# Moving the results of two expert quads by one block in a mixture-of-experts stage

## The chip, the cores and the metric

The kernel runs on one core of a Trainium2 chip. The metric is the device time of one execution in microseconds; the kernel before has a median of 2238.95 us over 3 runs (2238.46 to 2247.0).

## The reference

The reference is one layer of an encoder over 2048 tokens of width 1024: projections, a gated DeltaNet and an attention mixer, an output projection, and then a mixture of 32 experts with a final layer norm. Only the experts matter here:

```
hid = silu(xb @ w1[e]) * (xb @ w3[e])      # per block of tokens of expert e, 1024 -> 256
ys  = (hid @ w2[e]) * row_w                # 256 -> 1024, times the token's weight
out = segment_sum(ys, row_tok)             # two experts per token are added up
x   = layer_norm(ALPHA * x + gt2 * out, ln2_g, ln2_b)
```

Each token has two experts of one of four groups, so there are 4096 rows of work, spread unevenly over the 32 experts.

## The kernel before, in words

All stages before the experts (projections, attention, recurrence, output projection, routing) are outside the change. Routing leaves, for each expert, a list of its tokens; d_x1 holds the residual into which the experts' results are added, and d_h the experts' input.

The expert stage (`experts`, line 2049) works on two kinds of places. A *block* is up to 128 tokens of one expert. There are 40 places for blocks: 14 lone ones (`singles`) and 13 pairs of blocks of one expert (`pairs`), in the order lone, pair, lone, pair and so on, so that block n is a lone one when n is 0 mod 3, the first of a pair at 1 and the second at 2. A *quad* is four experts with at most 32 tokens each, put side by side in 128 rows; there are `QS` = 3 quads.

`blocks` (line 1996) writes the order of all engines out by hand (`manual_schedule`); GpSimd (POOL) and the three compute engines follow it as it stands. In its step n it issues the gather of block n + 3 (`gather`), the first half of block n's hidden product (`block_hid` 0), the transpose of the gated product of block n - 1 (`block_gt`), splits of weights, the second half of the hidden product, its activation, the transposes of block n + 1's rows (`block_x`), more splits, and then the output product of block n - 1 (`block_y`) and its addition to d_x1 (`block_out`, line 1892). A split (line 67) turns a weight tile into a high and a low part, on ScalarE and VectorE; it frees the raw tile, and the weights of the unit after next are then requested on SP's queue (`load_unit`). A lone block has three splits in its step (two of w1/w3 for the next unit and one of its own w2), the first of a pair has one (its w2), the second of a pair has two.

The output product goes into `yo`, which has two PSUM buffers of half a row width; VectorE scales it into `ye`, which has two buffers for blocks and quads together (line 1887 for blocks, 1960 for quads). From `ye` an indirect DMA with addition goes to d_x1; all of these write the same tensor, so each waits until the one before has landed.

The parts of a quad hang in this order at steps that the list `QA` gives, three numbers per quad (`quads`, line 1967): the first half of the hidden product (line 1932), the second half with the activation, and the output (line 1959). From these follow: the gather of the quad's rows three steps before the first (`quad_x`), its transposes one step before (`quad_xt`), the transpose of the gated product one step behind the second (`quad_gt`), and two additions to d_x1 behind the output (`quad_out`, line 1963), the second of them in the step after. The four raw weight tiles `qraw` are single: w1/w3 of the first half, of the second half, w2, and then the next quad's first half go into the same tiles, each set requested on SP's queue in two portions of two experts, in the step of the part that used the tiles last and in the step behind it.

```
QA = (13, 18, 21, 24, 27, 30, 33, 36, 39)
QL = ((0, 1), (2, 3))
```

Functions:

Of the kernel before, what the change touches and what calls it, by code (L numbers as in the profile page):

```python
# [44 lines left out]
SB = 2 * NP + NS  # L45
POS = 80
FEW, QS = 32, 3
QA = (13, 18, 21, 24, 27, 30, 33, 36, 39)
QL = ((0, 1), (2, 3))
TD = (0, 2)  # L50

# [5 lines left out]
class Layer:  # L57
# [1909 lines left out]
    def quads(self):  # L1967
# [3 lines left out]
        def put(n, f, *a):  # L1971
            at.setdefault(n, []).append(lambda: f(*a))
# [6 lines left out]
        for q in range(QS):  # L1979
            n = QA[3 * q:3 * q + 3]  # L1980
            put(n[0] - 3, self.quad_x, q)
# [200 lines left out]
```

## Time and profile before

| what | value |
|---|---|
| median of 3 runs | 2238.95 us (2238.46 to 2247.0) |
| profiled execution | 2234.89 us |
| its span (first to last instruction) | 2233.0 us |
| mean granted TensorE clock | 0.961 |
| TensorE, VectorE, ScalarE, GpSimd busy | 90%, 73%, 56%, 38% |

Busy times come from one profiled execution. The expert stage lies from about 1707 us (first gathers) to 2179 us; behind it come the loads of d_x1 and the final layer norm, to the end. PE is TensorE, DVE is VectorE, ACT is ScalarE, POOL is GpSimd and SP the queue that loads weights; L and a number is a line of the kernel.

### The profile page before, as it was taken

What the parts mean: (1) busy time and instruction counts of PE and PEld (TensorE: products, weight loads), DVE (VectorE), ACT (ScalarE), POOL (GpSimd) and SP (SyncE); (2) the same over time, 40 slices, a digit from 0 to 9 for tenths busy, and PEclk for the clock granted to TensorE, in tenths of its full rate; (3) what the DMA queues carried; (4) which work ended last, traced back from release to release, by engine and by line L of the source; (5) the groups of instructions that cost most, each with busy time, mean ns of one, the idle gap of its engine ahead of it and who ended that gap; (6) DMA issues with size and microseconds to landing.
All of it is one profiled execution on the core that took longest, in us unless ns stands there. A gap on an engine that the chain in (4) does not pass through costs nothing. (4 is left out here: it accounts for less than half of the span.)

```text
span 2233.0 us, 43291 instructions
## 1 busy us (share of the span) xinstructions
PE 2018.3 (90%) x15381; PEld 1783.1 (80%) x15381; DVE 1632.6 (73%) x3379; ACT 1260.4 (56%) x3072; POOL 838.5 (38%) x925
## 2 busy tenths in 40 slices
PE   5899998999999999979899999999995999999960
PEld 3899998999988888868788899888784787676740
DVE  5687747388775888878788556799787777676737
ACT  4767755466753787767677443434433554454526
POOL 0311134321132347777777355401334343343320
PEclk8999999999999999999999999999996999999985
DMA  8445653445444765676752888754435799999967
GB/s 275 143 123 150 159 173 109 120 133 154 150 130 131 226 186 141 158 197 165 194 132 47 273 289 296 261 175 155 143 128 148 213 325 317 326 323 339 325 175 302
DMA packets 406940, 441.35 MB, mean 198 GB/s; under 512 B 79947, under 2 KB 331179, under 8 KB 405691
## 3 DMA queue, kind: packets, MB, share of 16 engines
q1 hardware_dynamic: 390491, 402.69, 58.4%
q0 software_dynamic: 13920, 33.71, 6.2%
q8 instruction: 123, 2.02, 0.4%
q10 hardware_dynamic: 2304, 2.10, 0.3%
q14 instruction: 102, 0.84, 0.1%
HBM read 352.15 MB, written 121.37 MB: 212 GB/s over the span
## 5 line engine op out<-in xcount | busy, mean ns | idle before, releaser
L72 PE MATMUL pj<-wh,hthi 128*128 128x256 f32 (+1 forms) x768 | 225.7, 294 | 2.7 <-DVE lnmv L221 2.7
L73 PE MATMUL pj<-wl,hthi 128*128 128x256 f32 (+1 forms) x768 | 220.3, 287 | 2.7 <-DVE wl L67 2.7
L72 PE MATMUL pj<-hthi,wh 128*128 128x260 f32 x768 | 222.5, 290 | 0.0
L74 PE MATMUL pj<-wh,htlo 128*128 128x256 f32 (+1 forms) x768 | 220.1, 287 | 1.2 <-DVE htlo L274 1.2
L67 DVE TENSOR_TENSOR ptl<-pt,pth 128x512 fp32r<-128x512 f32 x256 | 176.3, 689 | 59.8 <-ACT pth L66 58.7
L74 PE MATMUL pj<-hthi,wl 128*128 128x260 f32 x768 | 217.1, 283 | 0.0
L73 PE MATMUL pj<-htlo,wh 128*128 128x260 f32 x768 | 216.6, 282 | 0.0
L206 POOL TENSOR_TENSOR xa<-xa 128x512 f32<-128x512 f32 (+2 forms) x96 | 84.0, 875 | 349.5 <-ACT xa L204 332.1
L66 ACT CAST pth<-pt 128x512 fp32r<-128x512 f32 x256 | 150.3, 587 | 95.2 <-PE pt L883 92.3
L328 DVE SCALAR_TENSOR_TENSOR cacc<-pj,convw,cacc 128x256 f32<-128x256 f32 x384 | 184.0, 481 | 10.0
L874 ACT ACTIVATE p<-s,mx 128x512 f32<-128x512 f32 x256 | 176.8, 691 | 13.3 <-DVE mx L865 11.3
L862 DVE TENSOR_REDUCE mx<-s 128x1 f32<-128x512 f32 x256 | 175.3, 685 | 9.1 <-PE s L74 3.3
L1892 POOL DMA_INDIRECT d_x<-ye,tid x40 | 81.0, 2026 | 253.5 <-DMA d_x<-ye,tid 112.2
L72 PE MATMUL o<-pth,vh 128*128 128x256 f32 x512 | 166.3, 325 | 0.0
L883 PEld LDWEIGHTS pt<-ident,p 128*128 128x128 f32 x1024 | 125.8, 141 | 43.4 <-DVE ptl L67 13.0
L883 PE MATMUL pt<-ident,p 128*128 128x128 f32 x1024 | 156.8, 276 | 3.0 <-DVE ptl L67 2.6
L67 DVE TENSOR_TENSOR w13l<-raw,w13h 128x2048 fp32r<-128x2048 f32 x54 | 123.7, 2291 | 39.3 <-ACT w13h L66 35.5
L73 PEld LDWEIGHTS pj<-wl,hthi 128*128 128x128 f32 x768 | 148.2, 193 | 3.1 <-DVE wl L67 3.1
L72 PEld LDWEIGHTS pj<-wh,hthi 128*128 128x128 f32 x768 | 148.2, 193 | 3.1 <-issue 3.1
L74 PEld LDWEIGHTS pj<-wh,htlo 128*128 128x128 f32 x768 | 148.0, 193 | 1.9 <-DVE htlo L274 1.9
L74 PE MATMUL o<-pth,vl 128*128 128x256 f32 x512 | 145.1, 283 | 0.0
L73 PE MATMUL o<-ptl,vh 128*128 128x256 f32 x512 | 145.0, 283 | 0.0
(528 smaller groups left out, 6299.9 us busy)
## 6 DMA issues: line engine op xcount, KB each, us to landing
raw<-in_w_dram SPq DMA_DIRECT2D x116, 512.0 KB
raw<-in_w_dram SPq DMA_DIRECT2D x29, 1024.0 KB
sh<-d_sh SPq DMA_DIRECT2D x32, 768.0 KB
qraw<-in_w_dram SPq DMA_DIRECT2D x48, 512.0 KB
xa<-in_w_ada_dram SPq DMA_DIRECT2D x32, 512.0 KB
dr<-d_dir SPq DMA_DIRECT2D x32, 512.0 KB
wraw<-in_w_in_dram SPq DMA_DIRECT2D x96, 128.0 KB
qraw<-in_w_dram SPq DMA_DIRECT2D x12, 1024.0 KB
```

What stands on the lines that cost most here:

```text
L66: (copy or self.nc.scalar.copy)(hi, src)
L67: (engine or self.nc.vector).tensor_tensor(lo, src, hi, op=OP.subtract)
L72: mm(out, a[0], b[0], start=start, stop=False)
L73: mm(out, a[0], b[1], start=False, stop=False)
L74: mm(out, a[1], b[0], start=False, stop=stop)
L206: nc.gpsimd.tensor_tensor(w[:, :n], w[:, :n], w[:, n:2 * n], op=OP.add)
L328: nc.vector.scalar_tensor_tensor(acc, ps[:, j:j + BLK], self.convw[:, j, ct:ct + 1], acc, op0=OP.mult, op1=OP.add)
L862: nc.vector.tensor_reduce(mx[:, i:i + 1], ps, axis=AX.X, op=OP.max)
L874: self.nc.scalar.activation(p[:, i * 512:i * 512 + 512], ps[i], AF.Exp, bias=mx[:, 4:5], scale=scale, accum_out=sm[:, i:i + 1])
L883: nc.tensor.transpose(pt[:, i, t], self.P[u, t][0][:, (2 * g + i) * 128:(2 * g + i + 1) * 128], self.ident)
L1892: self.nc.gpsimd.indirect_dma_start(out=self.d_x1, out_offset=bass.IndirectOffsetOnAxis(ap=self.tid[:, self.col(i)], axis=0), in_=self.YE. ...
```

## The change

Only the list of steps differs:

```diff
-QA = (13, 18, 21, 24, 27, 30, 33, 36, 39)
+QA = (13, 18, 22, 25, 28, 31, 34, 36, 39)
```

Quad 0's output goes from step 21 to 22; quad 1's three parts from 24, 27, 30 to 25, 28, 31; quad 2's first part from 33 to 34, while its second part and its output stay at 36 and 39. What hangs on these steps (gathers, transposes, additions, weight requests) moves with them.

## Rows read from the trace of the kernel before

**Rows 1.** The page: engine busy time, and one of the costliest groups.
```profile
PE 2018.3 (90%) x15381; PEld 1783.1 (80%) x15381; DVE 1632.6 (73%) x3379; ACT 1260.4 (56%) x3072; POOL 838.5 (38%) x925
...
L67 DVE TENSOR_TENSOR w13l<-raw,w13h 128x2048 fp32r<-128x2048 f32 x54 | 123.7, 2291 | 39.3 <-ACT w13h L66 35.5
```

**Rows 2.** Windows: stretch, length, busy per engine (instructions), clock, DMA share, GB/s.
```profile
1720.00:1944.00 224.00, 211.01 (x1066) 168.82 (x1068) 172.29 (x176) 121.26 (x136) 79.29 (x42) 1.00 0.94 294
1944.00:2141.00 197.00, 188.93 (x990) 139.54 (x991) 131.37 (x140) 91.57 (x107) 68.45 (x37) 0.98 1.03 330
2141.00:2180.00 39.00, 18.48 (x90) 12.07 (x88) 12.23 (x15) 5.41 (x7) 9.31 (x6) 0.76 0.36 72
```

**Rows 3.** Timeline of POOL: start, duration, instruction, idle before with releaser.
```profile
1944.78 1.58 POOL L1892 DMA_INDIRECT d_x<-ye,tid  x1 [6.62 <-DVE ye L1887]
1953.70 1.57 POOL L1963 DMA_INDIRECT d_x<-ye,qtc  x1 [7.34 <-DMA d_x<-ye,tid]
...
1961.09 1.61 POOL L1963 DMA_INDIRECT d_x<-ye,qtc  x1 [2.10 <-DMA d_x<-ye,qtc]
1969.50 3.25 POOL L1892 DMA_INDIRECT d_x<-ye,tid  x1 [6.80 <-DVE xTl L67]
...
1980.43 1.58 POOL L1892 DMA_INDIRECT d_x<-ye,tid  x1 [6.31 <-DVE g L1867]
...
2050.76 1.57 POOL L1892 DMA_INDIRECT d_x<-ye,tid  x1 [6.24 <-DMA d_x<-ye,tid]
...
2141.15 1.56 POOL L1892 DMA_INDIRECT d_x<-ye,tid  x1 [8.86 <-DVE g L1867]
...
2161.86 1.55 POOL L1963 DMA_INDIRECT d_x<-ye,qtc  x1 [3.83 <-DMA d_x<-ye,tid]
2166.30 1.55 POOL L1963 DMA_INDIRECT d_x<-ye,qtc  x1 [2.89 <-DMA d_x<-ye,qtc]
2172.42 1.55 POOL L1892 DMA_INDIRECT d_x<-ye,tid  x1 [4.58 <-DMA d_x<-ye,qtc]
```

**Rows 4.** The chain that ended last: start, duration, what.
```profile
2141.15 38.19 DMA d_x<-ye,tid
```

**Rows 5.** Timeline of DVE: the scaling of results, blocks 20, 21, 29, 31, 36.
```profile
1943.09 1.41 DVE L1887 SCALAR_TENSOR_TENSOR ye<-yo,wb,gt 128x512 f32<-128x512 f32 x2
...
1959.52 1.40 DVE L1887 SCALAR_TENSOR_TENSOR ye<-yo,wb,gt 128x512 f32<-128x512 f32 x2
...
2047.24 1.40 DVE L1887 SCALAR_TENSOR_TENSOR ye<-yo,wb,gt 128x512 f32<-128x512 f32 x2
...
2075.92 1.41 DVE L1887 SCALAR_TENSOR_TENSOR ye<-yo,wb,gt 128x512 f32<-128x512 f32 x2 [1.61 <-DMA d_x<-ye,qtc]
...
2132.28 1.40 DVE L1887 SCALAR_TENSOR_TENSOR ye<-yo,wb,gt 128x512 f32<-128x512 f32 x2
```

**Rows 6.** Timeline of PE: a lone block's wait, quad outputs, block 35's begin, quad 2.
```profile
1879.04 0.50 PE L81 MATMUL hid<-w13h,xTl 128*128 128x512 f32 x1 [1.19 <-DVE xTl L67]
...
1943.89 6.43 PE L1959 MATMUL yo<-qraw,qgT 128*32 128x512 f32 x32 [4.81 <-DVE ye L1887]
...
2048.04 5.34 PE L1959 MATMUL yo<-qraw,qgT 128*32 128x512 f32 x32 [4.81 <-DVE ye L1887]
...
2095.43 0.39 PE L80 MATMUL hid<-w13h,xTh 128*128 128x512 f32 x1
...
2119.51 3.59 PE L1932 MATMUL qh<-qraw,xqT 128*32 128x512 f32 x26 [1.87 <-DMA qraw<-in_w_dram]
...
2150.76 3.64 PE L1959 MATMUL yo<-qraw,qgT 128*32 128x512 f32 x32
```

**Rows 7.** Timeline of SP: issue of weight loads, start, duration, count.
```profile
2088.07 8.74 SPq L1833 DMA_DIRECT2D qraw<-in_w_dram  x4
...
2098.67 9.74 SPq L1833 DMA_DIRECT2D qraw<-in_w_dram  x4
2108.78 9.13 SPq L1833 DMA_DIRECT2D raw<-in_w_dram  x4
```

## The prediction

> **What bounds the kernel now.** I read the page first: TensorE is busy 2018.3 of 2233.0 us [rows 1], so a change that closes TensorE gaps looks welcome. The diff moves work only inside the expert stage, so next I read the busy times by stretch [rows 2]. From 1944 to 2141 us TensorE works 188.9 of 197 us, VectorE 131.4, and the DMA share is 1.03; from 2141 to 2180 the DMA share falls to 0.36 and TensorE stops half-way. The stage does not end when TensorE ends; what runs on after it is the subject.
>
> Third, the timeline of GpSimd [rows 3]. Each block's weighted result is added into d_x1 by one indirect DMA (line 1892), each quad's by two (line 1963), and each of them waits until the one before has landed, because all write d_x1. Call them scatters and number them by block. Scatter 20 was released by VectorE's `ye` (1944.78). From there on it is the other way round. Block 21's result is ready at 1959.52 + 1.40 = 1960.92 [rows 5], its scatter goes at 1969.50 [rows 3], 8.6 us later. Block 29's is ready at 2048.64 and goes at 2050.76, 2.1 us later, which is as near as VectorE comes again; block 36's is ready at 2133.68 and goes at 2141.15, 7.5 us later. The chain of waits says the same of the end: a merged step of scatters runs from 2141.15 for 38.19 us, to 2179.34 [rows 4], and the final normalisation starts behind it. So from 1944.78 to 2179.34 there is an unbroken chain of 26 scatters (20 of blocks, 6 of quads), 234.6 / 26 = 9.0 us each. What the change is worth is read from this chain, not from TensorE.
>
> What a step of the chain costs is also in these rows: from 1953.70 to 1980.43, while weights stream, they follow each other by 7.4, 8.4 and 10.9 us; from 2161.86, when the DMA share is low, by 4.4 and 6.1 us, and the last takes 6.9 us [rows 2 to 4].
>
> **The change part by part.** Blocks go in threes: n = 0 mod 3 is a lone block, n = 1 the first and n = 2 the second of a pair. Nothing is added or removed; every part keeps its instructions. quad 0's result goes from n = 21 to 22, all of quad 1 (24, 27, 30) one later, quad 2's first part from 33 to 34, its second part (36) and result (39) stay.
>
> *The two results.* At n = 21 TensorE sits idle 4.81 us before line 1959 and then needs 6.43 us for 32 matmuls; at n = 30 it is 4.81 and 5.34 us; at n = 39, undisturbed, the same 32 take 3.64 us [rows 6]. The idle time ends with VectorE's `ye`: in a lone block VectorE must do three splits of 2.29 us [rows 1] and gets to `ye` late (1943.09 [rows 5]), and until then both `yo` buffers are full. In the first block of a pair there is one split. There `ye` starts at 1959.52 [rows 5], and one half is out 0.7 us later, so a quad result put behind it waits some 0.5 us. TensorE gains (4.81 + 6.43 - 3.64 - 0.5) + (4.81 + 5.34 - 3.64 - 0.5) = 7.1 + 6.0 = 13.1 us.
>
> *What this uncovers.* In lone blocks without quad work TensorE waits for `xTl` before line 81, 1.19 us in the row shown and 1.12 to 1.13 us in three more like it [rows 6]. At n = 21, 24, 27, 30 and 33 a quad's matmuls now stand there and hide it; the change moves them to a block where VectorE isn't late. 5 x 1.15 = 5.8 us come back. Net for TensorE: 13.1 - 5.8 = 7.3 us less.
>
> *What of it reaches the end.* Block 20's `ye` is not touched, so scatter 20 goes at 1944.78 as before. Block 21's result would be ready some 10 us earlier (4.81 + 6.43 less 1.15), at 1951, but scatter 20 lands at about 1953.5, when the quad's first scatter now goes [rows 3]. The chain then holds scatter 21, quad, quad, 22 in place of quad, quad, 21, 22: the same three steps in another order, 10.9 + 7.4 + 8.4 us by the rows, and scatter 22 at 1980.4 in both. From then on TensorE can be ahead only as far as the two `ye` buffers let it; VectorE already waits 1.61 us for a quad's scatter at 2075.92 [rows 5]. So I book 0 of the 7.3 us. If that cover is gone (the chain is not what binds), it is -7.3.
>
> Here a rule of the Trainium skill speaks against me. Its page "Perfetto Trace Analysis", section "Optimization Strategy", says to look for the gaps on the most contended engine and to remove what blocks it there. TensorE is that engine by busy time, and by the rule the change would bring -7.3 us where the chain of rows gives 0. The trace bears the rule out as to the gaps, not as to what they delay.
>
> *The loads on SP's queue.* Those of quad 1 and the first ones of quad 2 move with the blocks that use them, at the same distance; the gathers of the quads' rows and GpSimd's queue too. On SP they now come after the one w2 load of a first block and after the four of a second block, and no longer behind the lone block's five: the bytes are the same, 0. The exception is quad 2's second set of w1/w3 weights. It was issued with n = 33 and 34 and used at 36; now with n = 34 and 35, still used at 36. Before: four loads from 2088.07 (8.74 us), four from 2098.67 (9.74 us) [rows 7], and TensorE waited for the last of them until 2119.51 [rows 6], 11.1 us after the issue ended. After: the buffers come free when the first part's matmuls end in n = 34, about 2095.5: block 35's first matmul begins at 2095.43 [rows 6], and the 3.64 us of the quad's first part only move from n = 33 to 34 ahead of it; then four quad loads, the four unit loads that went at 2108.78 (9.13 us), and the last four quad loads. Upper bound: 12 loads at the pace of those rows, 8.74 + 9.13 + 9.74 = 27.6 us, and 11.1 us to land: 2134, 15 us later than before. Lower bound: 12 x 0.524 MB at the 330 GB/s of the stretch [rows 2] is 19.1 us: 2114.6, 5 us earlier than before and no wait left. I take 2125, near the middle, since the queue had 9 us to drain while no quad load was on it: TensorE starts block 37 some 5.5 us later. Block 36's scatter has 7.5 us of slack, so the chain still doesn't see it. What it does see is that the last quad's w2 loads, issued behind line 1932 of n = 36, run 5.5 us later, beside scatters 36 and 37, which then take the busy 9 us in place of what they took: I estimate +2 us.
>
> **Sum.** 0 (chain for chain) + 0 (loads moved alike) + 2 = +2 us. The span of 2233.0 becomes 2235, the profiled execution 2234.89 becomes 2236.9. The median of the runs, 2238.95, lies 4.06 us above the profiled execution; with that, 2241. Bounds on the same: -13.1 to +12 (the far ends of the two rivals below).
>
> **Rivals.** *TensorE binds.* If the scatter chain only follows TensorE, all 7.3 us are cashed and the median is 2231.7; if the 1.15 us waits do not come back, 13.1 us and 2225.9. For it: TensorE is busy 96% of 1944 to 2141 [rows 2], the clean idle gaps, and a lag of only 2.1 us at block 29. Against it: after 1944.78 every scatter went at least 2.1 us after its own result was ready, the quads' too. This is the case in which the page's rule above holds.
>
> *Quad 2's weights come late.* At the upper bound, TensorE is 15 us later at block 37. It decides from 7.5 us on, where block 36's scatter has no slack left. The last quad's matmuls, 2150.76 to 2154.40 [rows 6], then end at about 2169.4, its result is ready 1.4 us later at 2171; two quad scatters of 4.4 and 6.1 us and the last block's of 6.9 us [rows 3, 4] end at 2188.5, against 2179.34: +9, so 2248 for the median; with 3 us more of congestion 2251, +12. For it: TensorE waits for these very loads already with a block more of lead. Against it: the queue drains beforehand, and TensorE is held back by the chain anyway.
>
> *The chain itself is cheaper or dearer.* Weight loads in other blocks change which scatters run beside them. A mean step of 9.0 us changed by 3% over 26 steps is 7 us either way.
>
> **Chances.** About what a measurement of this kernel can tell from no change is 0.5%, 11.2 us: faster is under 2227.8, slower over 2250.1. My forecast (2237 to 2245) 0.5; TensorE binds 0.22, of which 0.10 lies under 2227.8; late weights 0.18, of which 0.10 lies over 2250.1; a chain of another pace 0.10, split between all three. That makes 0.15 faster, 0.70 same, 0.15 slower. The range of 2226 to 2253 holds the first rival's far end and most of the second.
>
> **What would show it.** Right: idle before line 1959 under 1 us at n = 22 and 31 and its 32 matmuls near 3.7 us; waits of 1.1 us before line 81 in blocks 21 to 33; scatter 21 at about 1953.7, the quad's two behind it, scatter 22 near 1980; from there every scatter released by the one before. The first four late quad loads are issued at about 2095, the last four behind the unit loads, and line 1932 in n = 36 waits some 9 us in all. Wrong: scatters released by `ye` again after 1980 (then TensorE sets the pace), a chain whose steps differ by more than 3% from 9.0 us, or line 1932 waiting over 12 us.

## The result, and the profile after

The kernel with the change takes 2256.12 us (median of 10 runs, 2251.12 to 2265.2), the kernel before 2243.43 us (10 runs, 2235.26 to 2249.5). The ratio is 1.0077, 95% interval 1.0062 to 1.0092: by it the change costs some 17 us (13.9 to 20.6); the two medians lie 12.7 us apart. Forecast was +2 us, a median of 2241 within 2226 to 2253. The rival "Quad 2's weights come late" came true; by the ratio it was dearer than the +9 to +12 us at which it was priced.

The profiled execution after (2263.99 us, span 2262.2) is one of the long ones of the ten. Its first scatter goes at 1746.21, that of before at 1736.95, though nothing ahead of it was changed; a second profile of the kernel before (experiment b2_before) has it at 1738.25. So I compare stretches of the expert stage from the first scatter on, and subtract 9.26 us where a time of after is set beside one of before.

The page, the line that answers to [rows 1]:

```profile
PE 2031.9 (90%) x15381; PEld 1791.2 (79%) x15381; DVE 1634.5 (72%) x3379; ACT 1258.0 (56%) x3072; POOL 839.8 (37%) x925
```

The windows after, with the columns of [rows 2], from this profile's scatter 20 (1956.14) on; the first stretch is again 197 us long:

```profile
1956.00:2153.00 197.00, 168.01 (x861) 120.60 (x863) 119.87 (x126) 80.12 (x92) 68.19 (x37) 0.93 0.98 310
2153.00:2166.00 13.00, 13.00 (x66) 9.04 (x59) 5.75 (x8) 4.40 (x7) 0.00 (x0) 0.96 0.78 299
2166.00:2209.00 43.00, 24.44 (x128) 17.25 (x126) 15.93 (x19) 9.88 (x12) 9.29 (x6) 0.84 0.32 61
```

Within 197 us TensorE did 861 instructions in place of 990 [rows 2]: the stage got new idle time. The timeline of TensorE shows where (a choice of its rows: start, duration, instruction, count, idle before with releaser):

```profile
1949.84 0.50 PE L81 MATMUL hid<-w13h,xTl 128*128 128x512 f32 x1 [1.12 <-DVE xTl L67]
...
1959.64 3.64 PE L1959 MATMUL yo<-qraw,qgT 128*32 128x512 f32 x32 [0.40 <-DVE ye L1887]
...
1987.05 1.94 PE L1922 MATMUL tr<-ident,xq 128*128 128x128 f32 x8 [4.85 <-DMA xq<-d_h,qtid]
...
2066.91 1.05 PE L1959 MATMUL yo<-qraw,qgT 128*32 128x512 f32 x4 [0.43 <-DVE ye L1887]
...
2071.00 1.04 PE L1959 MATMUL yo<-qraw,qgT 128*32 128x512 f32 x2 [3.04 <-DMA qraw<-in_w_dram]
...
2074.66 5.72 PE L1959 MATMUL yo<-qraw,qgT 128*32 128x512 f32 x26 [2.62 <-DMA qraw<-in_w_dram]
...
2111.20 3.64 PE L1932 MATMUL qh<-qraw,xqT 128*32 128x512 f32 x32
...
2144.93 1.88 PE L1932 MATMUL qh<-qraw,xqT 128*32 128x512 f32 x2 [10.23 <-DMA qraw<-in_w_dram]
...
2150.14 5.53 PE L1932 MATMUL qh<-qraw,xqT 128*32 128x512 f32 x26 [3.33 <-DMA qraw<-in_w_dram]
```

The first two rows are as forecast: the gap of 4.81 us and the slow 6.43 us at quad 0's result [rows 6] are gone (0.40 and 3.64), and the wait before line 81 is back. It is back in three of the five places that were forecast (1949.84, 2023.42 and 2057.07, 1.12 to 1.17 us); in the lone blocks' steps 24 and 33 a quad's transposes (line 1922) now stand in its place, and wait 4.85 and 1.35 us. The rest is new: a wait of 5.66 us for quad 1's w2 weights in step 31, and 13.56 us for quad 2's second set in step 36.

SP's queue, to be read beside [rows 7]:

```profile
2114.85 7.09 SPq L1833 DMA_DIRECT2D qraw<-in_w_dram  x4
2122.57 8.28 SPq L1833 DMA_DIRECT2D raw<-in_w_dram  x4
2131.25 8.50 SPq L1833 DMA_DIRECT2D qraw<-in_w_dram  x4
```

Quad 1's w2 on the same queue, in before and then in after (two portions of two loads, the lines with `qraw`):

```profile
2017.17 2.16 SPq L1836 DMA_DIRECT2D qraw<-in_w_dram  x2
2022.54 0.37 SPq L1836 DMA_DIRECT2D raw<-in_w_dram  x1
2023.29 1.12 SPq L1836 DMA_DIRECT2D qraw<-in_w_dram  x2
```

```profile
2038.07 2.58 SPq L1836 DMA_DIRECT2D qraw<-in_w_dram  x2
2044.31 13.64 SPq L1833 DMA_DIRECT2D raw<-in_w_dram  x4
2058.33 2.25 SPq L1836 DMA_DIRECT2D qraw<-in_w_dram  x2
```

GpSimd, the scatters of blocks 20 and 21, of quad 0, of blocks 22 and 35 to 37, to be read beside [rows 3] (the gathers between them are left out):

```profile
1956.14 2.71 POOL L1892 DMA_INDIRECT d_x<-ye,tid  x1 [6.39 <-DMA d_x<-ye,tid]
1967.57 1.57 POOL L1892 DMA_INDIRECT d_x<-ye,tid  x1 [7.38 <-DMA d_x<-ye,tid]
1977.24 1.56 POOL L1963 DMA_INDIRECT d_x<-ye,qtc  x1 [8.10 <-DVE ye L1887]
1985.11 2.67 POOL L1963 DMA_INDIRECT d_x<-ye,qtc  x1 [1.64 <-DMA d_x<-ye,qtc]
1994.83 1.58 POOL L1892 DMA_INDIRECT d_x<-ye,tid  x1 [7.05 <-issue]
...
2141.23 1.57 POOL L1892 DMA_INDIRECT d_x<-ye,tid  x1 [6.22 <-DMA d_x<-ye,tid]
2166.51 1.56 POOL L1892 DMA_INDIRECT d_x<-ye,tid  x1 [23.71 <-DVE ye L1887]
2178.45 1.55 POOL L1892 DMA_INDIRECT d_x<-ye,tid  x1 [10.38 <-DVE ye L1887]
```

The last chain of waits still ends in a merged step of scatters that begins with block 36's. But before it the chain now holds 15.44 us in which no DMA runs, and the row above puts them down to `ye`; in before, block 36's went 0.7 us after block 35's had landed [rows 4]:

```profile
2166.51 42.11 DMA d_x<-ye,tid
```

Reckoned from the first scatter of each profile to the first load of d_x1 behind the stage (us):

| stretch | before | b2_before | after |
|---|---|---|---|
| first scatter to scatter 20 | 207.8 | 209.6 | 209.9 |
| scatter 20 to 35 | 183.8 | 187.5 | 185.1 |
| scatter 35 to 36 | 12.6 | 10.0 | 25.3 |
| scatter 36 to the load | 38.4 | 40.9 | 42.3 |
| whole | 442.6 | 448.0 | 462.6 |

The added time lies in one step of the chain, from scatter 35 to 36, with some 2 to 4 us behind it. Up to scatter 35 nothing was won or lost that two profiles of the kernel before do not differ by.

### The profile page after: what moved, and what is told of

It is laid out like the page before. It is cut to its first block, busy times and chain, and to the rows that moved or that the text cites. A ratio compares the mean times of both kernels' runs of the same rounds, so it can differ in the third digit from the quotient of the medians.

```text
span 2262.2 us, 43290 instructions
## 1 busy us (share of the span) xinstructions
PE 2031.9 (90%) x15381; PEld 1791.2 (79%) x15381; DVE 1634.5 (72%) x3379; ACT 1258.0 (56%) x3072; POOL 839.8 (37%) x925
## 5 line engine op out<-in xcount | busy, mean ns | idle before, releaser
L874 ACT ACTIVATE p<-s,mx 128x512 f32<-128x512 f32 x256 | 176.6, 690 | 15.9 <-DVE mx L865 14.2
```

Of the source, the lines that this page charges most:

```text
L874: self.nc.scalar.activation(p[:, i * 512:i * 512 + 512], ps[i], AF.Exp, bias=mx[:, 4:5], scale=scale, accum_out=sm[:, i:i + 1])
```

## The experiments

Unless it says otherwise an edit is to the list of steps or of portions, and is made on the kernel after.

**e1_q2_first_34**: the kernel before with quad 2's first part alone moved.

```diff
-QA = (13, 18, 21, 24, 27, 30, 33, 36, 39)
+QA = (13, 18, 21, 24, 27, 30, 34, 36, 39)
```

> The kernel before with one number changed: quad 2's first part at 34 in place of 33; quads 0 and 1 as before. Theory A (quad 2's second set of weights is requested too late, and TensorE waits for it in step 36): the whole loss is here, ratio to before 1.005 to 1.009, line 1932 waits 10 to 15 us in all in step 36, the scatter of block 36 comes 10 us or more behind that of block 35 plus its usual 12. Theory B (moving quads 0 and 1 is what costs, by loads that stand behind a second block's unit loads and by the scatters' new order): ratio 0.998 to 1.002.

Measured: 1.0028 (1.0012 to 1.0045). TensorE waits 5.87 + 1.03 us for the second set; scatter 36 is released by `ye` at 2153.57, 20.3 us after scatter 35. So the move of this part costs time by itself, between the two theories, but only a third of the loss. Here the twelve loads are issued in 2.91, 4.99 and 4.41 us, where in after they took 7.09, 8.28 and 8.50. TensorE's rows:

```profile
2134.47 1.88 PE L1932 MATMUL qh<-qraw,xqT 128*32 128x512 f32 x2 [5.87 <-DMA qraw<-in_w_dram]
...
2137.38 5.33 PE L1932 MATMUL qh<-qraw,xqT 128*32 128x512 f32 x26 [1.03 <-DMA qraw<-in_w_dram]
```

**e2_q2_second_37**: the second part gets its block of lead back.

```diff
-QA = (13, 18, 22, 25, 28, 31, 34, 36, 39)
+QA = (13, 18, 22, 25, 28, 31, 34, 37, 39)
```

> The changed kernel with quad 2's second part at 37 in place of 36, so that its weights have as much lead as before; its output stays at 39. Theory A: the waits before line 1932 of quad 2 fall under 4 us; ratio to before 0.997 to 1.002. Theory B: still 1.006 to 1.009. If only the wait moves to quad 2's w2 weights (requested in steps 37 and 38, used at 39), line 1959 waits there and the ratio lies between.

Measured: 1.0009 (0.999 to 1.0029). The loss is gone, though a wait of 4.18 us stands before line 1932, now in step 37; scatter 36 goes 9.6 us behind 35, and 37 19.8 us behind 36. Quad 1's w2 is as late here as in after (3.19 + 2.58 us before line 1959 in step 31), and so it is in e3 below (3.27 + 1.77).

**e3_one_portion**: quad 2's second set requested whole in step 34, ahead of the unit loads.

```diff
-            load(n[0], q, 1)
+            if q == 2:
+                for cs in QL:
+                    put(n[0], self.quad_load, q, 1, cs)
+            else:
+                load(n[0], q, 1)
```

> The changed kernel with quad 2's second set of w1/w3 requested whole in step 34 (both portions), in place of half in 34 and half in 35 behind the unit loads of step 35. Theory A, with the second portion's place in SP's queue as the reason: the waits before line 1932 in step 36 fall from 13.6 us to under 5, ratio to before 0.999 to 1.004. If the sheer number of bytes in front of step 36 is the reason, the order changes nothing: waits stay over 10 us, ratio 1.006 to 1.009. Theory B: 1.006 to 1.009 with shorter waits at step 36.

Measured: 1.0017 (0.9998 to 1.0037). SP's queue and TensorE:

```profile
2114.25 15.92 SPq L1833 DMA_DIRECT2D qraw<-in_w_dram  x8
2130.55 8.51 SPq L1833 DMA_DIRECT2D raw<-in_w_dram  x4
```

```profile
2134.64 1.02 PE L1932 MATMUL qh<-qraw,xqT 128*32 128x512 f32 x2 [0.54 <-DMA qraw<-in_w_dram]
...
2140.12 5.29 PE L1932 MATMUL qh<-qraw,xqT 128*32 128x512 f32 x26 [4.46 <-DMA qraw<-in_w_dram]
```

Issue begins as late as in after (2114.25), but the four unit loads no longer stand in between: the last set lands at 2140.12 in place of 2150.14, and the wait falls from 13.56 to 5.0 us. Same steps, same bytes, another order on SP, and the ratio falls from 1.0077 to 1.0017: most of the loss is the order of the queue.

**e4_all_early**: every part of all quads two steps or so earlier.

```diff
-QA = (13, 18, 22, 25, 28, 31, 34, 36, 39)
+QA = (13, 16, 19, 22, 25, 28, 31, 34, 37)
```

> All three outputs with the first block of a pair, but earlier instead of later: steps 13, 16, 19, 22, 25, 28, 31, 34, 37, each part three steps behind the one before. Theory A (late weights alone are the loss; the place of an output is worth little since the scatters are a chain): no wait on quad weights over 2 us, ratio to before 0.994 to 1.000, with what is gained coming from the end, where the last scatters run without weight loads beside them. Theory B (an output with the first block of a pair costs by itself): over 1.003. If TensorE's gaps were worth their full 13 us: about 0.994 or lower, with TensorE's last matmul 13 us earlier.

Measured: 1.0033 (1.0013 to 1.0054), a miss. With three steps for each part the quads' weights are late in other places: 4.32 us at step 19, 4.30 at 25, 5.78 for w2 at 37. By itself the ratio would also fit the second theory, that an output with the first block of a pair costs something; e7 and e9 below have all outputs there and lose nothing that can be measured.

**b2_before**: the kernel before once more, for a second profile.

> The kernel before once more, with a second profile, to see how far one profile of it differs from another outside the expert stage and in it. Both theories: ratio 1.00; if the profiled run shown at first was a low one, its first scatter (1736.95) and its stage (442.6 us from the first scatter to the first load of d_x1) come out some us longer here, and the stage lengths of the experiments have to be read against both.

Measured: 0.999 (0.9969 to 1.0012). The stage is 5.4 us longer than in the first profile, and TensorE waits 4.21 us for quad 2's second set in place of 3.26 (1.39 + 1.87). A difference of this size between two profiles proves nothing, and the forecast was built on the better of the two.

**e5_pe_7us** and **e6_pe_22us**: how much lateness of TensorE the end bears. The kernel before, with matmuls added behind step 36 that compute nothing that is used (`reps` 2 and 6):

```diff
+    def more_pe(self, reps):
+        w = self.xqT.rearrange("p a b -> p (a b)")
+        for j in range(8 * reps):
+            for c in range(4):
+                p = slice(32 * c, 32 * c + 32)
+                self.nc.tensor.matmul(self.qh[p], self.xqT[:, j % 8, p], w[:, 0:512], start=True, stop=True)
...
+        put(36.5, self.more_pe, 2)
```

> The kernel before with 64 more matmuls of the quads' shape (2 x 3.64 us) on TensorE in step 37, ahead of block 36's output product; their result goes nowhere. No load is moved. Theory A (the scatters are the chain and block 36 has 7.5 us of slack): scatter 36 is still released by scatter 35, ratio 0.999 to 1.002. Rival (TensorE sets the pace there): 1.003, with scatter 36 released by its own result.

> The same with 192 matmuls (21.8 us), as long as the delay that TensorE had in the changed kernel at that place. Theory A: 7.5 us of it are hidden; scatter 36 some 14 us later and released by its result, the end 10 to 16 us later: ratio 1.0045 to 1.007, near to the changed kernel's 1.0077. If that loss came from the weights' traffic and not from TensorE's delay: under 1.003. If TensorE sets the pace throughout: 1.010.

My expectations mis-sized the dose: each such matmul appears as two instructions, so TensorE was delayed by 13.94 and 41.41 us. The row of e5 and its scatter of block 36:

```profile
2135.44 13.94 PE L1940 MATMUL qh<-xqT 128*32 128x512 f32 x128
```

```profile
2153.40 1.56 POOL L1892 DMA_INDIRECT d_x<-ye,tid  x1 [20.93 <-DVE ye L1887]
```

Measured: 1.0062 (1.0042 to 1.0083) and 1.0171 (1.0145 to 1.0197), which on 2240.02 us are +13.9 us (9.4 to 18.6) and +38.3 us (32.5 to 44.1). A slack of 7.5 us would have left 6.4 and 33.9; the first lies outside its interval. By e5 the slack is between 0 and 4.5 us. The two profiles say the same: from scatter 35 to the load it takes 64.1 and 90.8 us in place of 51.0, so of 13.94 and 41.41 us only 0.8 and 1.6 are hidden. This is what the rival of both expectations said: at this end of the stage a delay of TensorE passes nearly in full.

**e7_after_whole**: all sets requested in one portion, so that each goes ahead of the next unit's loads.

```diff
-QL = ((0, 1), (2, 3))
+QL = ((0, 1, 2, 3),)
```

> The changed kernel with every set of quad weights requested whole in the step of the part that frees the tiles, not half of it one step later: quad 1's w2 then comes ahead of step 29's unit loads, quad 2's second w1/w3 ahead of step 35's. Theory A (what is late stands behind a second block's unit loads): the waits before line 1959 in step 31 (5.7 us) and before line 1932 in step 36 (13.6 us) fall to under 2 and under 6 us, ratio 0.997 to 1.002. If unit weights become late instead, TensorE waits at lines 80 to 83 and the ratio is over 1.004.

Measured: 1.0005 (0.9979 to 1.003). No weights are late at line 1959 of step 31 (the wait is 0.43 us, for `ye`), and 8.25 us are left at step 36, where under 6 were expected. As fast as before within 0.3%, with all steps where the change put them.

**e8_before_whole** is the same edit on the kernel before, **e9_whole_37** is e7 with the second part of quad 2 at 37.

> The kernel before with every set of quad weights requested whole, in the step of the part that frees the tiles. Its waits for quad weights (3.3 us before line 1932 in step 36) should go; in a lone block's step the whole set now stands ahead of the next w2 load. Theory A (only late weights in steps 35 and 36 count, and before they are late by little): 0.997 to 1.001. If an undivided set delays unit weights: over 1.002.

> The changed kernel with whole sets and quad 2's second part at 37: no quad weights should be late before the last w2. Theory A (late weights were the whole loss, and the scatter chain swallows what TensorE gains): waits before lines 1932 and 1959 under 3 us in all, ratio 0.997 to 1.001. Rival (the closed gaps are worth their 7 to 13 us once no weights are late): 0.994 to 0.997.

Measured: 0.9992 (0.9973 to 1.0012) and 1.0007 (0.999 to 1.0024): no change. In e8 1.34 us of the wait before line 1932 are left. In e9 that wait is down to 1.11 us, but w2 comes 4.44 us late at step 39, so the two make 5.55 us where under 3 were expected. TensorE's 7 us do not reach the end in either; these two runs alone do not say where they go.

**e10_after_whole_no_qout**, **e11_before_no_qout**, **e12_whole_37_no_qout**, **e13_before_whole_no_qout**: is it the chain that hides TensorE's gain? Kernels e7, before, e9 and e8, each with the four additions of quads 0 and 1 to d_x1 left out, which takes four scatters from the chain and nothing from TensorE:

```diff
-            for c in range(2):
+            for c in range(2 if q == 2 else 0):
```

> The changed kernel with whole sets, and the four additions of quads 0 and 1 to d_x1 left out (their results are computed and dropped). Theory A (TensorE's gain at the outputs is swallowed by the chain of scatters, each quad taking two steps of some 8 us in it): with these steps gone the gain shows, 10 to 18 us under the kernel before (ratio 0.992 to 0.9955), and at least 5 us faster than the kernel before without the same additions. Rival (the gain is eaten by the waits in lone blocks, by VectorE or by weights): no faster than that one.

> The kernel before with the four additions of quads 0 and 1 to d_x1 left out, as the partner of the last. Theory A: TensorE and the gaps before line 1959 then set the pace, 0 to 9 us faster than before (0.996 to 1.000), since the chain's lag of 2 to 12 us behind TensorE is all that can go. Rival (the chain alone binds): up to 30 us faster (0.987).

> e9 (outputs at 22 and 31, whole sets, quad 2's second part at 37) with the four additions of quads 0 and 1 left out: neither a chain that lags nor late weights. Theory A (the closed gaps are worth some 6 us on TensorE, and both the chain and the late weights hide or eat that): from scatter 20 to scatter 35 some 167 us, 5 to 7 us less than in e13, and 4 to 10 us faster than e13 in time. Rival (the waits in lone blocks or VectorE eat it): within 3 us of e13.

> e8 (the kernel before with whole sets) with the same four additions left out, as the partner of e12. Both theories: from scatter 20 to scatter 35 about 173 us as in e11, ratio to before 0.995 to 0.999.

Measured: 1.0004 (0.9989 to 1.002), 0.9985 (0.9969 to 1.0002), 0.9966 (0.9948 to 0.9983), 0.9956 (0.994 to 0.9972), each against the full kernel before. By total time the new places win nothing even here: e10 was expected at least 5 us faster than e11, and e12 4 to 10 us faster than e13, and neither is. By stretches (us):

| from scatter 20 | quads' places | to 33 | to 35 | 35 to the load |
|---|---|---|---|---|
| e11 | before | 151.1 | 172.8 | 58.2 |
| e13 | before | 151.5 | 173.9 | 52.5 |
| e10 | after | 144.7 | 169.7 | 65.7 |
| e12 | after | 142.7 | 167.7 | 59.7 |
| before, after, e7, e9 | | 161.8, 163.0, 162.3, 162.1 | | |

Scatters 20, 33 and 35 of e13, then of e12, as GpSimd's timeline has them:

```profile
1944.70 1.59 POOL L1892 DMA_INDIRECT d_x<-ye,tid  x1 [6.62 <-DVE ye L1887]
...
2096.16 1.58 POOL L1892 DMA_INDIRECT d_x<-ye,tid  x1 [6.52 <-DVE ye L1887]
...
2118.57 1.58 POOL L1892 DMA_INDIRECT d_x<-ye,tid  x1 [6.71 <-DVE g L1939]
```

```profile
1949.82 2.59 POOL L1892 DMA_INDIRECT d_x<-ye,tid  x1 [6.50 <-DMA d_x<-ye,tid]
...
2092.54 1.58 POOL L1892 DMA_INDIRECT d_x<-ye,tid  x1 [6.51 <-DMA d_x<-ye,tid]
...
2117.53 1.59 POOL L1892 DMA_INDIRECT d_x<-ye,tid  x1 [6.62 <-DVE ye L1887]
```

With the full chain all four kernels need the same 162 to 163 us to scatter 33. With four scatters fewer those with the new places are quicker than their partners by 6.4 us (e10 against e11) and 8.7 us (e12 against e13). Scatter 20 goes 2.4 us after its result in e11 and e12 and at once in the other two; from block 20's result to block 33's it is 9.0 and 7.8 us. So the gain on TensorE is real, near the 7.3 us that was booked for it, and the chain hides it up to there. One way in which it does so shows on GpSimd: in after the gather of quad 1's rows goes at 1979.10, right behind quad 0's first scatter (1977.24), and TensorE waits 4.85 us for it before line 1922. In e10 and e12, without that scatter, this wait is 1.34 and 1.45 us, and it is for `xTl`. Behind scatter 35 both give the gain back. In e10 quad 2's second set is late, and in e12 quad 2's w2 in step 39:

```profile
2149.05 1.04 PE L1959 MATMUL yo<-qraw,qgT 128*32 128x512 f32 x2 [2.78 <-SPq L2071]
2151.57 6.57 PE L1959 MATMUL yo<-qraw,qgT 128*32 128x512 f32 x26 [1.48 <-SPq L2071]
```

## Why the prediction was wrong

**The two results, the uncovered waits, and the chain: right.** The gaps closed, the 1.1 us waits came back in three places of five, and TensorE's transposes (line 1852) of step 22 lie at 1955.45, in before's time 1946.19, against 1956.13 in before: the "some 10 us earlier" of the text. The order scatter 21, quad, quad, 22 came as forecast, though scatters 21 and 22 came some 5 us later than said (in before's time 1958.31 and 1985.57, where 1953.7 and 1980 were said). From scatter 20 to 22 it took 38.7 us in place of 35.6 (1944.78 to 1980.43 [rows 3]), and to 35 185.1 in place of 183.8. So the 0 for the chain holds up to scatter 35, and e10 to e13 put the rival "TensorE binds" out for that stretch. That scatters would follow only each other was too strong: of blocks 26, 28 and 29 `ye` released them again. This was one of the text's own signs of being wrong; another was line 1932 waiting over 12 us, and it came too (13.56).

Here the rule of the Trainium skill (page "Perfetto Trace Analysis", section "Optimization Strategy") to close the gaps on the most contended engine can be weighed. The gaps at quad 0's and quad 1's results are closed in e7 too (0.41 and 0.43 us are left), and its ratio is 1.0005; but e7 still waits 8.25 us at step 36, so the stretch from scatter 20 to 33, ahead of that wait, is the better test: 162.3 us in e7 and 161.8 in before. There the rule did not pay, since a chain of DMAs and not the busiest engine set the pace; with four scatters left out it did (142.7 us in e12, 151.5 in e13).

**"The loads moved alike cost 0": wrong for quad 1's w2.** Before, TensorE did not wait for these weights. After, the first portion was issued 11.6 us later than in before (2038.07 - 9.26 against 2017.17), which is about one step; the second 25.8 us later (2058.33 - 9.26 against 2023.29). It now stood behind the four loads of a second block of a pair, which took 13.64 us from 2044.31, where in before one load of 0.37 us stood there. TensorE waited 5.66 us, and the 32 matmuls took 7.81 us in place of the 3.64 that were booked. TensorE's transposes of steps 31 and 32, in before and then in after, show what it cost:

```profile
2059.14 1.04 PE L1852 MATMUL tr<-ident,xg 128*128 128x128 f32 x8
...
2068.46 1.04 PE L1852 MATMUL tr<-ident,xg 128*128 128x128 f32 x8
```

```profile
2062.71 1.03 PE L1852 MATMUL tr<-ident,xg 128*128 128x128 f32 x8
...
2086.17 1.04 PE L1852 MATMUL tr<-ident,xg 128*128 128x128 f32 x8
```

In before's time TensorE was 5.7 us ahead at step 31 and 8.5 us behind at step 32. Of these 14.2 us some 4 are quad 1's output itself, which in before lies ahead of both rows; the wait and the slow matmuls make the other 9.8. At step 35 TensorE was 10.2 us behind (2120.60 - 9.26 against 2101.13). e7, where the portion goes ahead of those loads, has no such wait.

**Quad 2's second set: the step that failed.** The text said that the tiles come free at "about 2095.5", that the last load lands at 2125, that "TensorE starts block 37 some 5.5 us later" and that "Block 36's scatter has 7.5 us of slack, so the chain still doesn't see it". Measured, in before's time: the tiles came free at 2105.58 (2111.20 + 3.64 - 9.26), 10.1 us later than said. From there to the last landing it took 35.3 us (2114.84 to 2150.14) where I had 29.5, inside my bounds of 19 to 38.5. The last 26 matmuls took 5.53 us in place of 3.59 [rows 6]. Together with the 5.5 us booked that is 10.1 + 5.8 + 1.9 + 5.5 = 23.3 us, and TensorE did end the part 23.3 us later (2155.67 - 9.26 against 2123.10). The upper bound of 15 us was no bound, since it kept the moment at which the tiles come free.

**The slack was read at the wrong scatter.** 7.5 us is block 36's lag behind its own result; in b2_before it is 1.5 us. Block 37's is 4.1 us in the first profile, and 0.3 us in b2_before; once 36 is late, 37 follows at TensorE's pace (11.9 us after it, and no longer 8.5). At most the least of the lags behind the delay is slack. e5 gives 0 to 4.5 us. 23.3 less 4.1 is 19.2 us; in the profile after the first load behind the stage comes 20.0 us later (2208.83 - 9.26 against 2179.56), and the ratio gives 17 (13.9 to 20.6). The +2 us that were booked behind scatter 36 fit what was measured there (1.5 to 3.9 us), but by luck: block 37's scatter waited for its own result, not for a busy DMA.

**Two causes that seem to need each other.** Quad 2's move alone (e1) costs 0.28%, everything else with the lead restored (e2) 0.09%; both together 0.77%. The excess of 0.40% is more than the three intervals leave to chance (some 0.3%), but not by much. Quad 1's late w2 by itself is borne: e2 and e3 have it, with 5.0 to 5.8 us of waiting, and lose 0.09 and 0.17%. With that w2 in time, and quad 2's second set still 8.25 us late, e7 loses 0.05%. The kernel after with quad 1's w2 alone requested whole, which would part the two cleanly, was not run.

**What stays open.** Why b2_before's stage is 5.4 us longer than before's, and what is left of 0.05 to 0.17% in e2, e3 and e7, which is less than the runs can tell from nothing. What the wait of 4.85 us for quad 1's rows (line 1922, step 24) costs in time was not tried by itself; e7 and e9 have it too (4.97 and 5.30 us).

## What to carry to other kernels

A weight request that moves by one step keeps its distance in steps but not its place in the queue: list, in order, everything that the queue holds between request and use, at the old place and at the new one. When a transfer starts on the release of a tile, an earlier lateness is added to it in full, so bound the moment of release too, and not the transfer alone. Slack against a late engine is at most the smallest lag of all later links of the chain; read it in more than one profile. A chain that hides what an engine gains does not therefore hide what it loses: here 7 us of gain vanished in it, and of a delay of 13.94 us nearly all came out.

## What the runs showed of the hardware

TensorE can come out of a wait for weights slow. Windows after, around the second set of quad 2 (columns of [rows 2]):

```profile
2137.00:2144.90 7.90, 0.00 (x0) 0.01 (x1) 2.12 (x3) 0.00 (x0) 1.57 (x1) 0.50 1.07 322
2144.90:2150.10 5.20, 1.88 (x2) 0.17 (x2) 0.00 (x0) 0.00 (x0) 0.00 (x0) 0.50 0.99 304
2150.10:2155.70 5.60, 5.56 (x27) 1.31 (x27) 0.00 (x0) 0.00 (x0) 0.00 (x0) 0.65 0.22 90
2155.70:2162.00 6.30, 6.30 (x32) 5.20 (x33) 1.75 (x3) 2.93 (x4) 0.00 (x0) 1.00 0.95 354
```

While it waits the granted clock is 0.50, the 1.2 GHz level; the 26 matmuls that follow run at a mean of 0.65 and take 5.53 us where before they took 3.59 at 1.00; the next stretch is back at 1.00. The late w2 of step 31 had the same tail (5.72 us), and in other runs the 26 of line 1932 took from 5.21 us (e6) to 6.50 us (e5). So a wait of this kind costs 1.6 to 2.9 us more than the idle time that its row shows. Not every wait does: in before, e8 and e9, with 3.26, 1.34 and 1.11 us of waiting ahead of them, the same 26 took 3.59 us.

The last load of quad 2's second set landed 10.4 us after its issue on SP ended in after (2139.75 to 2150.14), with the DMA share near 1, 10.0 us in e3, 11.1 us in e1 and in before [rows 6, 7], and 8.0 us in b2_before, whether four loads took 4.41 us to issue (e1) or eight took 15.92 (e3). It was not always so: the last of quad 1's w2 in after landed 14.1 us after its issue ended (2060.58 to 2074.66).
